# Two transformer blocks in one kernel: inputs loaded by features, the normalization applied after the first projections, another order of the in-projections

## The chip, the cores and the metric

The kernel runs on one core of a Trainium2 chip. A core has five engines that work side by side, each with its own in-order queue: TensorE (PE; the loading of its stationary operand is listed as PEld), VectorE (DVE), ScalarE (ACT), GpSimd (POOL) and SyncE (SP, which here only issues DMAs). The metric is the device time of one execution in microseconds. The same program before the change takes 843.48 us in the median of three runs (843.4 to 843.89).

## What is computed

Two transformer blocks on one sequence of 256 positions with 1024 features, all in float32. In the first block a Mamba-style branch (`ssd`) and a gated linear recurrence (`lru`) are fed from one in-projection, then follows a convolutional feed-forward stage. The second block has a delta-rule branch, a spatial gating branch, a sliding-window attention and an attention to a memory of 256 rows. Cut to what the change touches:

```python
def rmsnorm(x, w):
    y = x * rsqrt(mean(x * x, -1) + 1e-6)
    return y * w

def first_block(x, ...):
    h = rmsnorm(x, mix_pre_norm)
    u_z, u_xbc, u_dt, u_ly, u_lx, u_g = split(h @ w_in)
    y_a = ssd_mixer(u_z, u_xbc, u_dt, ...)     # conv, scan, times silu(u_z), grouped norm
    y_b = rglru_mixer(u_ly, u_lx, ...)         # recurrence over conv(u_lx), times gelu(u_ly)
    g = sigmoid(u_g + gate_b)
    x = x + rmsnorm((g0 * (y_a @ w_proj_ssm) + g1 * (y_b @ w_proj_lru)) @ w_out, ...)
    ...                                        # feed-forward
def second_block(x, mem, ...):
    cols = rmsnorm(x, norm_pre) @ w_in_2
    mem_kv = rmsnorm(mem, norm_mem) @ w_mem_kv
    # delta branch: q, k are divided by their norm over the 128 features of a head;
    # in chunks: solve (I + L) u = rhs with L strictly lower triangular
    ...
```

## The kernel before

**Precision.** Every big product is done in three passes on numbers split into a high and a low part (`mm3`: high by high, high by low, low by high). The weights come from memory as halves of 512 KB (`Weights`): `load` brings one into one of three raw buffers, `_split` lets ACT cast it to the high part (`whi`, L112) and DVE subtract that for the low part (`wlo`, L113), into one of five pairs of buffers. Activations are kept by features (features on the partitions, positions along the free dimension), as `HH` and `HL`.

**Projections.** `proj_fm` makes 256 output features for all 256 positions: 48 matmuls of 256 columns. `proj_tm` makes 512 output features by positions: 48 matmuls of 512 columns. A projection asks for its weights with `W.next`, which also splits the halves up to five ahead. The PSUM pool `pp` has four banks for them.

**The order of PE.** `block1` and `block2` are the main program. It yields after each 12 matmuls of 256 columns or 6 of 512 columns. `Weave` counts these yields as steps, and after each lets one side program (two in the second block) put its next piece of PE work in between. A side program yields either a number of steps to wait, or the name of an event and a number of steps behind it; `yield "name"` in the main program is a join, which forces whatever is left of a side program at once. So PE's order is written out by hand, step by step. ACT's and DVE's order is chosen by the framework's planner, except inside `manual_schedule` in `program()`, where it is as written. SP's order is the planner's too.

**Start.** `program()` normalizes X by positions into `h0` (`norm_tm`: squares on ACT, root, reciprocal, scaling on DVE), transposes it with 16 PE transposes (`to_fm`) and evicts each feature tile into `HH` (ACT, times the norm's weight) and `HL` (DVE). In the same stretch it splits the first five weight halves, and casts the small weights (`small_w`).

**Block 1.** The in-projections run in the order `xbc` (4, 5, 0 to 3), `z`, `lx`, `ly`, then the gates `g0` to `g3`. Beside them run the side programs: `side_dt`; `side_ssd`, which transposes x (`pxt`), waits for the event `z`, and then makes a decay matrix (`pe`, three Exp on ACT) and every second step two heads (`py`); `side_gn`, the grouped norm, after `ssd` and `z`; `side_lru`, from the event `ssd` on, with eight pairs of products `pg` that read the buffer `lw`. The bias `gb` of the gates is loaded into that same buffer once the last `pg` has read it, and DVE adds it to each gate tile as it evicts it (L905). `side_mem` normalizes, transposes and splits the memory input while `pb` runs.

**Block 2.** `side_delta` sums the squares of q and k with four groups of `pss` products (one column each), makes `L` (`pkk`), and calls `diagonal()`: POOL inverts the diagonal blocks of 32 by 62 small instructions, with DMAs to memory and back to re-lay them before and after. `yield 30` then leaves 30 steps to it before the products `pit`, `piy`, `pix` (the doubling of the blocks), `pvn`, `pS`, `pr`, `pq` and `po1`. The main program joins `delta` behind the gates `g230` and `g231`, ahead of the product `up3`.

The lines that matter most for what follows:

```python
            diagonal()
            yield 30
...
                if p == 3:
                    yield ("z", 1)
...
            if p == 3:
                gb = big.tile([P, 2 * D], F32, tag="lw", name="gb")
                with tc.issue_after(W.loaded.ins):
                    nc.sync.dma_start(gb, gbias)
```

Of the kernel before, what the change touches and what calls it, by code (L numbers as in the profile page):

```python
# [8 lines left out]
F32 = mybir.dt.float32  # L9
# [57 lines left out]
class Weights:  # L67
# [48 lines left out]

    def next(self, kt=8):
# [63 lines left out]
def two_blocks_kernel(  # L181
    ctx: ExitStack,
    tc: tile.TileContext,
    x: bass.AP,
    mem: bass.AP,
    pcol: bass.AP,
# [73 lines left out]
    nc.sync.dma_start(wsmall, wsm.rearrange("p (k c) -> p k c", k=8))  # L260
    W.load(3)
    pr = cp.tile([P, NROW], F32, name="pr")
    nc.sync.dma_start(pr, prow)
# [304 lines left out]

    lamc = COL["lru_lambda"]
# [14 lines left out]
    def side_dt():  # L584

        yield 7
# [33 lines left out]
    def side_ssd():  # L620
# [42 lines left out]
        for h in range(-4, 18):  # L663
            if h < 0:
                p = h + 4
                yield (f"xs{p}", 7)

                pt = bank(f"pxt{p}")
                for tt in range(2):
                    for i in range(2):  # L670
                        nc.tensor.transpose(
                            pt[:, tt * S + i * P : tt * S + (i + 1) * P],
                            XS[:, 2 * p + i, tt * P : (tt + 1) * P], ident)
                for tt in range(2):
# [12 lines left out]
            yield 1  # L687
# [64 lines left out]
    def side_gn():  # L752
# [3 lines left out]
        SZ = ya["sz"]  # L756
        sq = tmp("gnsq")
# [40 lines left out]
    def side_mem():  # L798
# [7 lines left out]
        EL = act8("b5", "EL", F32R)  # L806
        for tt in range(2):
# [53 lines left out]
    def block1(HH, HL):  # L861

        for p in (4, 5, 0, 1, 2, 3):
            ps, _ = yield from proj_fm(f"xbc{p}", HH, HL, p == 4)
# [30 lines left out]
        wv.event("ly")  # L895
# [99 lines left out]
    def block2(HH, HL, MK, MV):  # L995
# [127 lines left out]
        def side_delta():  # L1123

            for a in range(2):
                for p in range(2):
                    yield (f"dn{a}{p}", 10)
                    sq = sqs[a, p]
                    pss = bank(f"pss{a}{p}")
                    for j in range(2):  # L1130
                        for tt in range(2):
                            i = 2 * j + tt
                            nc.tensor.matmul(pss[:, i : i + 1], sq[:, j, tt * P : (tt + 1) * P],
                                             one[:, 0:1], start=True, stop=True)
                    nc.vector.tensor_copy(
                        rn[:, a, :, 2 * p : 2 * p + 2],
                        pss[:, 0:4].rearrange("p (j t) -> p t j", j=2))
# [48 lines left out]
            yield 30  # L1186
# [424 lines left out]
    def program():  # L1611
        h0 = big.tile([P, 2, D], F32, tag="b2", name="h0")
# [15 lines left out]
    with tc.manual_schedule(engines={nc.tensor.engine}):  # L1628
        wv.add("dt", side_dt())
# [9 lines left out]
    "x", "mem", "pcol", "prow", "wsm", "lruw", "wsT", "lvl", "post", "gbias", "w_in", "w_pa", "w_pb",  # L1639
# [4 lines left out]
def _layout(inp):  # L1644
# [15 lines left out]
    d = {"x": a("x")[0], "mem": a("mem_2")[0]}  # L1660
    d["post"] = np.stack([
# [20 lines left out]
    d["w_in"] = np.concatenate([xbc, tiles(wz), tiles(wlx), tiles(wy), tiles(wg, 512)])  # L1682
# [80 lines left out]
```

## Time and profile before

| | before |
|---|---|
| median of three runs | 843.48 us |
| profiled execution, its own time | 844.04 us |
| span of the profiled execution | 842.3 us |
| mean granted TensorE clock | 0.993 |
| PE busy | 819.2 us, 97% |
| PEld busy | 749.4 us, 89% |
| DVE busy | 593.8 us, 70% |
| ACT busy | 511.9 us, 61% |
| POOL busy | 53.4 us, 6% |
| read from memory | 142.84 MB, 171 GB/s over the span |

The span runs from the first to the last instruction of the core; an execution's own time is a little longer. A busy share is an average over the whole span: an engine with 70% can still be the one that is late in a stage. The granted clock is the share of the full TensorE clock of 2.4 GHz that the chip allowed; 0.50 of it is 1.2 GHz. Matmuls are pipelined: one takes 0.28 us from start to end while the next starts 0.12 us behind it, so what counts is the distance of the starts.

### The profile page before, as it was taken

What the parts mean: (1) busy time and instruction counts of PE and PEld (TensorE: products, weight loads), DVE (VectorE), ACT (ScalarE), POOL (GpSimd) and SP (SyncE); (2) the same over time, 40 slices, a digit from 0 to 9 for tenths busy, and PEclk for the clock granted to TensorE, in tenths of its full rate; (3) what the DMA queues carried; (4) which work ended last, traced back from release to release, by engine and by line L of the source; (5) the groups of instructions that cost most, each with busy time, mean ns of one, the idle gap of its engine ahead of it and who ended that gap; (6) DMA issues with size and microseconds to landing.
All of it is one profiled execution on the core that took longest, in us unless ns stands there. A gap on an engine that the chain in (4) does not pass through costs nothing.

```text
span 842.3 us, 14020 instructions
## 1 busy us (share of the span) xinstructions
PE 819.2 (97%) x5464; PEld 749.4 (89%) x5464; DVE 593.8 (70%) x973; ACT 511.9 (61%) x777; POOL 53.4 (6%) x97
## 2 busy tenths in 40 slices
PE   6999999999999999999999999999779999999997
PEld 5999899888889999999889899998779988888886
DVE  6896974996778788888743787766545666466673
ACT  7675768884556655655643478856736665544452
POOL 0000000000000000000000100048710000000000
PEclk9999999999999999999999999999979999999999
DMA  7755344656754665565665464454604346666551
GB/s 247 260 168 159 121 151 126 203 192 207 253 169 152 206 194 179 176 196 179 207 194 195 132 227 143 152 159 127 178 10 150 104 148 200 200 200 195 181 199 51
DMA packets 40387, 145.07 MB, mean 172 GB/s; under 512 B 4673, under 2 KB 4929, under 8 KB 40065
## 3 DMA queue, kind: packets, MB, share of 16 engines
q1 hardware_dynamic: 39600, 142.73, 53.2%
q0 software_dynamic: 576, 0.92, 0.6%
q8 instruction: 43, 0.70, 0.3%
q10 hardware_dynamic: 144, 0.52, 0.2%
q14 instruction: 24, 0.19, 0.1%
HBM read 142.84 MB, written 1.31 MB: 171 GB/s over the span
## 4 chain that ended last, share of the span: by engine, by line
PE 89%; POOL 5%; DMA 2%; DVE 2%; issue 1%; ACT 1%; DVEq 0%; POOLq 0%
PE fu L399 5%; PE fu L398 5%; PE fu L400 5%; PE g L398 5%; PE g L399 5%; PE g L400 5%; PE z L398 3%; PE fd L398 3%; PE fd L399 3%; PE fd L400 3%; PE z L399 2%; PE z L400 2%; POOL bM L1113 2%; POOL bM L1109 2%; PE up L399 2%; PE up L398 2%
## 5 line engine op out<-in xcount | busy, mean ns | idle before, releaser
L113 DVE TENSOR_TENSOR wlo<-wraw,whi 128x1024 fp32r<-128x1024 f32 x258 | 314.9, 1227 | 153.1 <-ACT whi L112 151.1
L112 ACT CAST whi<-wraw 128x1024 fp32r<-128x1024 f32 x258 | 268.7, 1050 | 218.1 <-PE fu L399 48.5
L398 PE MATMUL fu<-HH,whi 128*128 128x256 f32 x384 | 108.7, 283 | 0.0
L399 PE MATMUL fu<-HL,whi 128*128 128x256 f32 x384 | 108.7, 283 | 0.0
L400 PE MATMUL fu<-HH,wlo 128*128 128x256 f32 x384 | 108.7, 283 | 0.0
L398 PE MATMUL g<-whi,HH 128*128 128x512 f32 x192 | 75.9, 395 | 0.0
L400 PE MATMUL g<-whi,HL 128*128 128x512 f32 x192 | 74.8, 390 | 0.0
L399 PE MATMUL g<-wlo,HH 128*128 128x512 f32 x192 | 74.7, 389 | 0.0
L398 PEld LDWEIGHTS fu<-HH,whi 128*128 128x128 f32 x384 | 73.7, 192 | 0.0
L399 PEld LDWEIGHTS fu<-HL,whi 128*128 128x128 f32 x384 | 73.7, 192 | 0.0
L400 PEld LDWEIGHTS fu<-HH,wlo 128*128 128x128 f32 x384 | 73.7, 192 | 0.0
L398 PE MATMUL z<-HH,whi 128*128 128x256 f32 x192 | 57.2, 298 | 0.0
L399 PE MATMUL z<-HL,whi 128*128 128x256 f32 x192 | 54.7, 285 | 0.0
L400 PE MATMUL z<-HH,wlo 128*128 128x256 f32 x192 | 54.7, 285 | 0.0
L560 DVE SCALAR_TENSOR_TENSOR fc<-fu,pc,fc 128x255 f32<-128x255 f32 (+1 forms) x96 | 43.7, 478 | 1.6
L400 PEld LDWEIGHTS g<-whi,HL 128*128 128x128 f32 x192 | 36.0, 188 | 7.6
L398 PEld LDWEIGHTS g<-whi,HH 128*128 128x128 f32 x192 | 36.1, 188 | 7.3
L399 PEld LDWEIGHTS g<-wlo,HH 128*128 128x128 f32 x192 | 36.1, 188 | 7.3
L399 PE MATMUL fd<-wlo,FH 128*128 128x512 f32 (+1 forms) x120 | 41.7, 347 | 0.0
L398 PE MATMUL fd<-whi,FH 128*128 128x512 f32 (+1 forms) x120 | 41.6, 347 | 0.0
L400 PE MATMUL fd<-whi,FL 128*128 128x512 f32 (+1 forms) x120 | 41.6, 347 | 0.0
L398 PEld LDWEIGHTS z<-HH,whi 128*128 128x128 f32 x192 | 37.2, 194 | 0.8 <-issue 0.7
(522 smaller groups left out, 2026.2 us busy)
## 6 DMA issues: line engine op xcount, KB each, us to landing
wraw<-in_w_in_dram SPq DMA_DIRECT2D x130, 512.0 KB, 3.9
wraw<-in_w_fu_dram SPq DMA_DIRECT2D x48, 512.0 KB, 3.8
wraw<-in_w_fd_dram SPq DMA_DIRECT2D x24, 512.0 KB, 3.8
wraw<-in_w_o_dram SPq DMA_DIRECT2D x16, 512.0 KB, 3.9
wraw<-in_w_up_dram SPq DMA_DIRECT2D x16, 512.0 KB, 3.5
wraw<-in_w_pa_dram SPq DMA_DIRECT2D x8, 512.0 KB, 3.5
wraw<-in_w_pb_dram SPq DMA_DIRECT2D x8, 512.0 KB, 4.4
wraw<-in_w_mk_dram SPq DMA_DIRECT2D x4, 512.0 KB, 4.2
```

Of the source, the lines that this page charges most:

```text
L112: nc.scalar.copy(hi, raw)
L113: nc.vector.tensor_tensor(out=lo, in0=raw, in1=hi.bitcast(F32), op=ALU.subtract)
L398: nc.tensor.matmul(o, wh, xh, start=first, stop=False)
L399: nc.tensor.matmul(o, wh, xl, start=False, stop=False)
L400: nc.tensor.matmul(o, wl, xh, start=False, stop=last)
L560: nc.vector.scalar_tensor_tensor(o[:, d:S], in0=p[:, 0 : S - d], scalar=col(wname, (taps - 1 - d) * n + i), in1=o[:, d:S], op0=ALU.mult, o ...
L1109: eng.tensor_tensor(out=t, in0=xb[:, j : j + 1, :].to_broadcast([P, n, 8]), in1=lb[:, j, j + 1 : 32].unsqueeze(2).to_broadcast([P, n, 8]), ...
L1113: eng.tensor_tensor(out=xb[:, j + 1 : 32, :], in0=xb[:, j + 1 : 32, :], in1=t, op=ALU.subtract)
```

## The change

The layout on the host adds X and the memory input a second time, by features (`xT`, `memT`, two halves each).

- **Start.** X by features comes first, each half followed by a weight half; X by positions, most of the column constants, the small weights and the row constants come behind them (`more_loads`). The first two weight halves are split in four pieces each (`split_pieces`), and behind each piece one feature tile of X, not normalized, is multiplied with the norm's weight and split into `HU` and `LU` (`feature`). The squares of X by positions follow behind the fourth half, and give the factor of each position.
- **Order of block 1.** The four `ly` projections come first, made from `HU` and `LU`; the factor is applied to their result, when they are evicted (DVE, times `rbc`). The new side program `side_rms` spreads the factors over the partitions with two small matmuls into `rbc`, and DVE multiplies X by features with it in four steps, each followed by the split of two feature tiles into `HH` and `HL`. All later projections use those.
- **ssd, z.** The heads of `side_ssd` no longer wait for the event `z`; z is evicted with a plain copy and Silu is applied in `side_gn`.
- **Memory.** `side_mem` loads the memory by positions (for the squares) and by features; two small matmuls spread the factors, POOL multiplies (two feature tiles at a time), ACT and DVE split. The transposes go.
- **Norms on quarters.** The sums of squares of four heads are made by four matmuls on 32-column quarters of the array, copied and transposed.
- **Doubling later.** `yield 30` becomes `yield 44`.

```diff
+    def split_pieces(self, n):
...
+        for i in range(n):
+            q = slice(i * w, (i + 1) * w)
+            nc.scalar.copy(hi[:, q], raw[:, q])
+            nc.vector.tensor_tensor(out=lo[:, q], in0=raw[:, q], in1=hi[:, q].bitcast(F32),
+                                    op=ALU.subtract)
+            yield
+        self.load(j + 1 + self.raw_bufs)
...
-    nc.sync.dma_start(X[:, 0, :], x[0:P, :])
-    nc.scalar.dma_start(X[:, 1, :], x[P : 2 * P, :])
     pc = cp.tile([P, NCOL], F32, name="pc")
-    nc.sync.dma_start(pc, pcol)
-    W.load(2)
+    nc.scalar.dma_start(pc[:, 0:8], pcol[:, 0:8])
+    XT = act8("b2", "XT")
+    for g in range(2):
+        nc.sync.dma_start(XT[:, 4 * g : 4 * g + 4, :],
+                          xT[g].rearrange("p (k t) -> p k t", k=4))
+        W.load(g + 1)
+    W.load(3)
...
+    def more_loads(i):
+        if i == 0:
+            for tt in range(2):
+                nc.sync.dma_start(X[:, tt, :], x[tt * P : (tt + 1) * P, :])
+        else:
+            nc.sync.dma_start(pc[:, 8:NCOL], pcol[:, 8:NCOL])
+            nc.sync.dma_start(wsmall, wsm.rearrange("p (k c) -> p k c", k=8))
+            nc.sync.dma_start(pr, prow)
...
+    def feature(k, src, hi, lo):
+        w = col("mix_pre_norm", k)
+        nc.scalar.activation(hi[:, k, :], src[:, k, :], AF.Identity, scale=w)
+        nc.vector.scalar_tensor_tensor(
+            lo[:, k, :], in0=src[:, k, :], scalar=w, in1=hi[:, k, :].bitcast(F32),
+            op0=ALU.mult, op1=ALU.subtract)
...
+    def side_rms():
+        yield 6
+        ps = bank("prx")
+        for tt in range(2):
+            nc.tensor.matmul(ps[:, tt * P : (tt + 1) * P], rx[:, tt : tt + 1].to_broadcast([P, P]),
+                             ident, start=True, stop=True)
+        nc.scalar.copy(rbc, ps[:, 0:S])
+        wv.event("rms")
+        y = act8("b7", "xn")
+        for g in range(4):
+            yield 1
+            q = slice(2 * g, 2 * g + 2)
+            nc.vector.tensor_tensor(out=y[:, q, :], in0=XT[:, q, :],
+                                    in1=rbc.unsqueeze(1).to_broadcast([P, 2, S]), op=ALU.mult)
+            for k in (2 * g, 2 * g + 1):
+                feature(k, y, HH, HL)
+        wv.event("h")
...
     def side_dt():
-        yield 7
+        yield ("h", 5)
...
                 if p == 3:
-                    yield ("z", 1)
+                    yield 1
...
         SZ = ya["sz"]
+        for hf in range(2):
+            q = slice(4 * hf, 4 * hf + 4)
+            nc.scalar.activation(SZ[:, q, :], SZ[:, q, :], AF.Silu)
...
+        MT = act8("b0", "MT")
+        for g in range(2):
+            nc.sync.dma_start(MT[:, 4 * g : 4 * g + 4, :],
+                              memT[g].rearrange("p (k t) -> p k t", k=4))
...
-            norm_tm(MEM[:, tt, :], MEM[:, tt, :], f"mem{tt}")
-        yield 10
-        yield from to_fm(MEM, EH, EL, "norm_mem_2", "mem", 1)
+            nc.scalar.activation(MEM[:, tt, :], MEM[:, tt, :], AF.Square,
+                                 accum_out=rm[:, tt : tt + 1])
...
+                nc.gpsimd.tensor_tensor(out=MT[:, q, :], in0=MT[:, q, :],
+                                        in1=rmb.unsqueeze(1).to_broadcast([P, 2, S]), op=ALU.mult)
...
     def block1(HH, HL):
+        late = []
+        for p in range(4):
+            ps, b = yield from proj_fm(f"ly{p}", HU, LU, p == 0)
+            late.append((p, ps, b))
+            while late and "rms" in wv.events:
...
+            yield
+        wv.event("ly")
...
-            nc.scalar.activation(SZ[:, 2 * p : 2 * p + 2, :], b, AF.Silu)
+            nc.scalar.copy(SZ[:, 2 * p : 2 * p + 2, :], b)
...
             wv.event(f"lx{p}")
-            yield
-        for p in range(4):
-            _, b = yield from proj_fm(f"ly{p}", HH, HL)
-            nc.scalar.copy(GY[:, 2 * p : 2 * p + 2, :], b)
             if p == 3:
                 gb = big.tile([P, 2 * D], F32, tag="lw", name="gb")
...
         def side_delta():
-                for p in range(2):
-                    yield (f"dn{a}{p}", 10)
...
+                yield (f"dn{a}1", 10)
+                pss = bank(f"pss{a}")
+                for h in range(4):
+                    nc.tensor.matmul(pss[32 * h : 32 * h + 32, 0:S], one[:, 0:32],
+                                     sqs[a, h // 2][:, h % 2, :], start=True, stop=True,
+                                     tile_position=(0, 32 * h))
+                f = sm.tile([P, S], F32, tag="spf", name=f"ss{a}", bufs=1)
+                nc.vector.tensor_copy(f, pss[:, 0:S])
+                yield 3
...
             diagonal()
-            yield 30
+            yield 44
...
     def program():
...
-            for tt in range(2):
-                norm_tm(h0[:, tt, :], X[:, tt, :], f"n1{tt}", True)
-            W.split(1)
-            for _ in to_fm(h0, HH, HL, "mix_pre_norm", "n1", 0,
-                           lambda b: W.split((1, 2, 2, 4)[b])):
-                pass
+            for g in range(2):
+                for k, _ in enumerate(W.split_pieces(4)):
+                    feature(4 * g + k, XT, HU, LU)
+                more_loads(g)
+            W.split(4)
+            for tt in range(2):
+                nc.scalar.activation(NRM[:, 0:1024], X[:, tt, :], AF.Square,
+                                     accum_out=rx[:, tt : tt + 1])
+            nc.scalar.activation(rx, rx, AF.Sqrt, bias=eps1, scale=1.0 / D)
+            nc.vector.reciprocal(rx, rx)
```

## Rows read from the trace of the kernel before

**Rows 1.** The page, first part: busy us (share of the span) xinstructions

```profile
PE 819.2 (97%) x5464; PEld 749.4 (89%) x5464; DVE 593.8 (70%) x973; ACT 511.9 (61%) x777; POOL 53.4 (6%) x97
```

**Rows 2.** Timeline of PE: start us, us, engine, line, instruction, xcount [idle us before <-releaser]

```profile
7.97 3.39 PE L488 MATMUL n_t<-ident,h 128*128 128x128 f32 x16 [7.97 <-DVE h L478]
...
11.78 0.39 PE L399 MATMUL xbc<-HL,whi 128*128 128x256 f32 x1 [0.31 <-DVE HL L498]
...
615.09 1.94 PE L1200 MATMUL pit<-bXY,bLA 128*128 128x64 f32 x8 [8.67 <-DMA bXY<-dx]
```

**Rows 3.** Windows: us, busy us of PE, PEld, DVE, ACT, POOL, granted clock, DMA share, GB/s

```profile
610.00:612.00 2.00, 0.00 (x0) 0.00 (x0) 0.00 (x0) 0.00 (x0) 0.30 (x1) 0.93 0.35 143
620.00:622.00 2.00, 2.00 (x11) 1.56 (x11) 0.00 (x0) 0.00 (x0) 0.00 (x0) 0.52 0.00 0
```

**Rows 4.** Timeline of PE, 256-column matmuls early and behind the hole

```profile
12.47 0.28 PE L398 MATMUL xbc<-HH,whi 128*128 128x256 f32 x1
12.59 0.28 PE L399 MATMUL xbc<-HL,whi 128*128 128x256 f32 x1
...
619.17 0.41 PE L398 MATMUL z<-HH,whi 128*128 128x256 f32 x1
619.38 0.41 PE L399 MATMUL z<-HL,whi 128*128 128x256 f32 x1
```

**Rows 5.** Timeline of POOL, first and last DMA round of the solve

```profile
550.29 2.47 POOL L1097 DMA_DIRECT2D dl<-bLA  x4 [62.30 <-DVE XPB L1431]
...
611.70 2.33 POOL L1121 DMA_DIRECT2D bXY<-dx  x4 [4.47 <-DMA dx<-bM]
```

**Rows 6.** Chain that ended last: start us, us, what (one fp32 matmul may be two records)

```profile
82.16 0.80 PE py L655 x8
...
226.94 0.87 PE mem_t L488 x8
...
507.96 0.79 PE pss L1133 x8
...
540.61 0.92 PE pkk L1170 x4
```

**Rows 7.** Timeline of POOL, two instructions of the solve, 144 columns each

```profile
582.17 1.29 POOL L1109 TENSOR_TENSOR bM<-bM,bXY 128x144 f32<-128x144 f32 x1
583.54 0.50 POOL L1113 TENSOR_TENSOR bM<-bM 128x144 f32<-128x144 f32 x1
```

**Rows 8.** Timeline of DVE: a weight split, low parts of features, 512 columns

```profile
9.51 1.22 DVE L113 TENSOR_TENSOR wlo<-wraw,whi 128x1024 fp32r<-128x1024 f32 x1
...
11.25 1.66 DVE L498 SCALAR_TENSOR_TENSOR HL<-n_t,pc,HH 128x256 fp32r<-128x256 f32 x4 [0.52 <-ACT HH L496]
...
114.62 0.68 DVE L761 TENSOR_TENSOR XS<-XS,SZ 128x512 f32<-128x512 f32 x1
```

**Rows 9.** Timeline of ACT: the first square of X, high parts of features

```profile
5.63 1.06 ACT L465 ACTIVATE h<-X 128x1024 f32<-128x1024 f32 x1 [2.90 <-DMA X<-in_x_dram]
...
10.38 1.57 ACT L496 ACTIVATE HH<-n_t,pc 128x256 fp32r<-128x256 f32 x4 [0.96 <-PE n_t L488]
```

**Rows 10.** Windows, columns as in rows 3: the first loads

```profile
3.00:6.00 3.00, 0.00 (x0) 0.00 (x0) 0.20 (x2) 0.37 (x1) 0.00 (x0) 1.00 1.00 399
```

**Rows 11.** Windows, columns as in rows 3: the stage of the xbc projections

```profile
30.00:40.00 10.00, 10.00 (x83) 9.89 (x83) 9.75 (x20) 7.24 (x9) 0.00 (x0) 1.00 0.89 315
```

**Rows 12.** Timeline of PE: the first matmuls of gate projection g2

```profile
164.62 0.39 PE L398 MATMUL g<-whi,HH 128*128 128x512 f32 x1
164.85 0.39 PE L399 MATMUL g<-wlo,HH 128*128 128x512 f32 x1
```

**Rows 13.** Timelines of SP and DVE: the load of gb, its first use

```profile
152.52 0.33 SPq L893 DMA_DIRECT2D gb<-in_gbias_dram  x1
...
158.82 1.28 DVE L905 TENSOR_TENSOR G<-g,gb 128x512 f32<-128x512 f32 x2
```

**Rows 14.** DMA issues: tensors, queue, xcount, KB each, median us to landing

```profile
gb<-in_gbias_dram SPq DMA_DIRECT2D x1, 1024.0 KB, 4.9
```

More of the change, by code (lines that the diff above doesn't have):

```diff
@@ L115, in _split @@
             self.ns += 1
+    def split_pieces(self, n):
+        nc, j, w = self.nc, self.ns, HW // n
+        raw = self.raw.pop(j)
+        hi = self.pool.tile([P, HW], F32R, tag="whi", name=f"whi{j}", bufs=self.bufs)
+        lo = self.pool.tile([P, HW], F32R, tag="wlo", name=f"wlo{j}", bufs=self.bufs)
+        self.hl[j] = (hi, lo)
+        self.ns += 1
+        for i in range(n):
[5 more added lines that the diff above has]
+        self.load(j + 1 + self.raw_bufs)
     def next(self, kt=8):
@@ L184, in two_blocks_kernel @@
     x: bass.AP,
+    xT: bass.AP,
     mem: bass.AP,
+    memT: bass.AP,
     pcol: bass.AP,
@@ L567, in two_blocks_kernel @@
     wv = Weave(1)
+    HU = act8("b3", "HU", F32R)
+    LU = act8("b6", "LU", F32R)
+    NRM = big.tile([P, 2048], F32, tag="b5", name="NRM")
+    rbc = NRM[:, 1024 : 1024 + S]
+    rx = sm.tile([P, 2], F32, name="rx", bufs=1)
+    def feature(k, src, hi, lo):
[21 more added lines that the diff above has]
+        wv.event("h")
     lamc = COL["lru_lambda"]
@@ L806, in side_mem @@
         EL = act8("b5", "EL", F32R)
+        rm = sm.tile([P, 2], F32, name="rm", bufs=1)
         for tt in range(2):
-            norm_tm(MEM[:, tt, :], MEM[:, tt, :], f"mem{tt}")
-        yield 10
-        yield from to_fm(MEM, EH, EL, "norm_mem_2", "mem", 1)
+            nc.scalar.activation(MEM[:, tt, :], MEM[:, tt, :], AF.Square,
+                                 accum_out=rm[:, tt : tt + 1])
+        nc.scalar.activation(rm, rm, AF.Sqrt, bias=eps1, scale=1.0 / D)
+        nc.vector.reciprocal(rm, rm)
+        yield 8
+        ps = bank("prm")
+        for tt in range(2):
+            nc.tensor.matmul(ps[:, tt * P : (tt + 1) * P], rm[:, tt : tt + 1].to_broadcast([P, P]),
+                             ident, start=True, stop=True)
+        rmb = MEM[:, 0, 0:S]
+        nc.scalar.copy(rmb, ps[:, 0:S])
+        for k in range(8):
+            w = col("norm_mem_2", k)
+            if k % 2 == 0:
+                q = slice(k, k + 2)
+                nc.gpsimd.tensor_tensor(out=MT[:, q, :], in0=MT[:, q, :],
+                                        in1=rmb.unsqueeze(1).to_broadcast([P, 2, S]), op=ALU.mult)
+            nc.scalar.activation(EH[:, k, :], MT[:, k, :], AF.Identity, scale=w)
+            nc.vector.scalar_tensor_tensor(
+                EL[:, k, :], in0=MT[:, k, :], scalar=w, in1=EH[:, k, :].bitcast(F32),
+                op0=ALU.mult, op1=ALU.subtract)
         em["h"], em["l"] = EH, EL
@@ L861, in block1 @@
     def block1(HH, HL):
+        late = []
[3 more added lines that the diff above has]
+            while late and "rms" in wv.events:
+                i, ps, b = late.pop(0)
+                o = GY[:, 2 * i : 2 * i + 2, :]
+                if b is not None:
+                    nc.vector.tensor_tensor(
+                        out=o, in0=b, in1=rbc.unsqueeze(1).to_broadcast([P, 2, S]), op=ALU.mult)
+                    continue
+                for j in range(2):
+                    nc.vector.tensor_tensor(out=o[:, j, :], in0=ps[j], in1=rbc, op=ALU.mult)
+            yield
+        assert not late
+        wv.event("ly")
         for p in (4, 5, 0, 1, 2, 3):
-            ps, _ = yield from proj_fm(f"xbc{p}", HH, HL, p == 4)
+            ps, _ = yield from proj_fm(f"xbc{p}", HH, HL)
             two = (2 * p, 2 * p + 1)
@@ L1125, in side_delta @@
             for a in range(2):
-                for p in range(2):
-                    yield (f"dn{a}{p}", 10)
-                    sq = sqs[a, p]
-                    pss = bank(f"pss{a}{p}")
-                    for j in range(2):
-                        for tt in range(2):
[L1132 to L1137, printed above, removed]
+                yield (f"dn{a}1", 10)
[7 more added lines that the diff above has]
+                yield 3
+                pst = bank(f"psst{a}")
+                for tt in range(2):
+                    t = slice(tt * P, (tt + 1) * P)
+                    nc.tensor.transpose(pst[:, t], f[:, t], ident)
+                nc.vector.tensor_copy(
+                    rn[:, a], pst[:, 0:S].rearrange("p (t h c) -> p t h c", t=2, c=32)[:, :, :, 0])
             sk, rq = rn[:, 0], rn[:, 1]
@@ L1628, in two_blocks_kernel @@
     with tc.manual_schedule(engines={nc.tensor.engine}):
+        wv.add("rms", side_rms())
         wv.add("dt", side_dt())
@@ L1638 @@
 _ARGS = (
-    "x", "mem", "pcol", "prow", "wsm", "lruw", "wsT", "lvl", "post", "gbias", "w_in", "w_pa", "w_pb",
+    "x", "xT", "mem", "memT", "pcol", "prow", "wsm", "lruw", "wsT", "lvl", "post", "gbias", "w_in", "w_pa", "w_pb",
     "w_o", "w_mk", "w_mv", "w_fu", "w_fd", "w_in2", "w_up2", "w_o2",
@@ L1660, in _layout @@
     d = {"x": a("x")[0], "mem": a("mem_2")[0]}
+    d["xT"] = d["x"].T.reshape(2, 4, P, S).transpose(0, 2, 1, 3).reshape(2, P, 4 * S)
+    d["memT"] = d["mem"].T.reshape(2, 4, P, S).transpose(0, 2, 1, 3).reshape(2, P, 4 * S)
     d["post"] = np.stack([
@@ L1681, in _layout @@
     xbc = tiles(wx)[[4, 5, 0, 1, 2, 3]]
-    d["w_in"] = np.concatenate([xbc, tiles(wz), tiles(wlx), tiles(wy), tiles(wg, 512)])
+    d["w_in"] = np.concatenate([tiles(wy), xbc, tiles(wz), tiles(wlx), tiles(wg, 512)])
     d["w_pa"] = tiles(a("w_proj_ssm")[0], 512)
```

5 lines of the change are left out of this document (removed).

## The prediction

> **What bounds the kernel now.** I read the page's first part: TensorE (PE) is busy for 819.2 us of a span of 842.3 us [rows 1], so only what PE waits for or no longer has to do can move the end. Then PE's timeline, for its idle rows. There are only two of size: 7.97 us ahead of its first instruction, and 8.67 us ahead of the matmul `pit` of the second block's delta side [rows 2]. Elsewhere the matmuls follow each other without a hole, so ScalarE (ACT), VectorE (DVE) and the weight loads keep up everywhere else. The second hole costs more than its length. The granted clock is 0.93 in 610 to 612 us and 0.52 in 620 to 622 us [rows 3]: between the levels of 2.4 and 1.2 GHz those shares mean that it falls near 611.7 and is back near 621.9 us. At the low level a 256-column matmul starts every 0.21 us, at the high one every 0.12 us [rows 4]. That `pit` waits for the small triangular solve on GpSimd (POOL) and its four rounds of DMA, which start at 550.29 us and whose last loads are issued at 611.70 us [rows 5]. PE runs through the 30 program steps (one `yield` of the main program each) that the code leaves for it between 550 and 606 us, 1.9 us a step.
>
> **The change, part by part.**
>
> (a) "Doubling later", 30 to 44 steps. Every later piece of the delta side comes 14 steps later. At 1.4 us (twelve 256-column matmuls of 0.12) to 1.9 us a step that is 20 to 27 us of other PE work, and 8.7 are wanted. So the hole goes: 8.67 us. With it goes the slow stretch behind it, 615.1 to 621.9 us: 6.8 x (1 - 0.12/0.21) = 2.9 us. Sum **11.6 us gained**. The cover is the z and gate projections, which are there anyway. What comes late next is the delta side's own end: counted step by step, its last product `po1` was due 11 steps ahead of the forced join in front of `up3`, and 14 steps later it is forced at the join, one step (1.4 us) behind `pvn1`. Between them DVE has to evict `pvn1` (512 columns, as in the 0.68 us row) behind at most one weight split of 1.22 us [rows 8]: **0.5 us lost**, 0 to 1.5.
>
> (b) The memory input loaded by features. Sixteen PE transposes go, two groups of 0.87 us [rows 6]; two full float32 matmuls of 128 columns come. A float32 matmul of 256 columns takes 0.43 us (two in the 0.92 us row less its overlap) [rows 6], so these take 0.21 us each. **Gain 1.3 us.** DMAs: SP issues 1 MB more (`MT`) behind `MEM`; weights are five halves ahead there, so nothing waits for it. POOL gets four multiplications of 128x512. In the solve two of its instructions of the same 144 columns take 0.50 and 1.29 us, 0.8 apart [rows 7]. So the new ones take 1.8 us each by width, up to 2.6, about 10 us in all; the split features are wanted 25 us later. Cost 0; if DVE loses the 0.8 us four times in return, 3 us, the five halves in hand still cover most of it, so at most 1. The Trainium skill ("SBUF — State Buffer", Who interferes with whom) says that a DVE instruction with two SBUF inputs and a GpSimd one that reads SBUF exclude each other for a whole instruction; the long row agrees with it. By that rule DVE could be held for most of the 10 us, and the sum would be 1 us worse or more.
>
> (c) Norms on quarters. Four groups of `pss`, 0.8 us each [rows 6], 3.2 us, go. In come, twice, four float32 matmuls of 256 columns on 32-column quarters of the array and two transposes (0.22 us). One after another the four take 1.7 us, side by side 0.43. The nearest row is `py`, four matmuls on 64-column halves, 0.80 us [rows 6] where the widths add up to 1.28: part of the overlap. I take 0.7. **Gain 3.2 - 1.8 = 1.4 us**, between -0.7 and 1.9. The Trainium skill ("TensorEngine Tiling (Array Packing)", Theoretical Speedup) states up to 4x for 32-column tiles. The `py` row falls short of the 2x that it states for halves. By the page the gain would be 1.9 us.
>
> (d) The start. Before, X (1.05 MB) lands at 5.6 us [rows 9], and the queue moves 399 GB/s from 3 us on [rows 10], 1.04 MB by then; then squares, scaling, transposes and eviction follow, and the stream proper starts at 11.8 us. After, X by features and the first weight half are 1.05 MB at the head of the queue: again 5.7 us. ACT and DVE then split k-slices in turn. A 128x256 piece takes ACT 0.4 us [rows 9] and DVE 0.4 [rows 8] in a row of four, two on each engine per slice, 0.75 us a slice. The first slice is complete at 7.0 us, the eighth at 12.3 us; PE begins on the first at 6.6 us. It starts at the low clock level (as the second hole shows it takes it some 6 to 7 us of work behind an idle stretch to get back, while before the change it had done so by 12 us, 4 us after its first transpose; I take 3.9 us): three slices at 6 x 0.21 = 1.28 us, the rest at 0.72 us. The first 48 matmuls end at 14.1 us instead of 11.8 + 48 x 0.12 = 17.6 us: **3.5 us gained**, if nothing follows. Three things follow. Two small matmuls for the row factors: 0.4 us. X by positions comes only behind the fourth weight half, which waits for the first one's split (9.1 us): 2 us until data flow and 1.6 MB at 399 GB/s make 15.2 us. ACT's written order then puts the second square (1.3 us), the root, the small weights and the Exp table load (3 us together, an estimate) ahead of the fifth half's cast, which ends near 20.5 us (1.0), its DVE part near 21.7 us (1.2, [rows 8]); projection `ly2` wants it at 20.4 us: 1.3 us. Then, from 20.6 us, DVE owes five weight splits (5.7), eight slices scaled (2.4) and split (3.0) and the late evictions (1.9), 13.0 us, and PE wants most of it by 32 to 33 us; DVE has 0.25 us free in 10 us of the next stage [rows 11]: 1.0 us, 0 to 4. **Net 0.8 us gained**, between -3 and 3.1.
>
> (e) LRU gate first. The projections `ly` go from the end of the in-projections to the front. So xbc, its events and the ssd side come 16 steps later. The ssd side regains 10 by no longer waiting for z, and starts 6 steps later than before, measured from the gate projections `g0` to `g3`, which stay in place. Its successors move by 6 as well: the eight `pg` products, and the load of `gb` into the buffer they read. Before, `gb` is issued at 152.52 us, right behind the last `pg`, lands 4.9 us later [rows 14], and DVE adds it to the first two gate tiles from 158.82 us, 0.6 us each [rows 13], which frees the PSUM bank that `g2` needs. `g2` starts at 164.62 us [rows 12], 5.1 us behind the first of them. Six steps of 1.37 us (six 512-column matmuls of 0.23, [rows 12]) are 8.2 us, so PE **waits 2.6 us**: 3.1 if DVE is as late as before, 1.8 if at once, and from 0 to 6 in all, since SP holds the later weights behind that load. The rest of the LRU chain had more room. z evicted without Silu saves ACT table swaps; the two wide Silus come in the same 13 us ahead of `pgn` and cost nothing if ACT runs them early. SP's other moved loads are in (d).
>
> **Sum**: 11.6 - 0.5 + 1.3 + 1.4 + 0.8 - 2.6 = 12.0 us. The profiled execution took 844.04 us (span 842.3 and 1.7 around it), 0.56 above the median of the runs: 832.0 on its footing, **831.5 us** on the median's.
>
> **The rivals.** A: the start runs clean and `gb` is hidden. Then (d) is 3.1 and (e) 0: 826.6 us. For it: PE tolerates lateness, five halves are in hand. Against: DVE at 9.75 of 10 us [rows 11]. B: the start is lost to DVE (-3) and the `gb` wait takes 5: 837.7 us. C: the change doesn't do what it says at `pit`: the hole reappears, with its slow clock, because POOL's chain stretches by as much as the 14 steps. Then only the small parts stay: 843.1 us. Against it: nothing is added to that chain. D, slower: the feed of the first projections is so thin that PE stays at the low level through all four `ly`. The point is a slice taking ACT and DVE over 1.28 us instead of 0.75; then 4 x 48 matmuls cost 0.09 us more each, 17 us, and the end is 849 us. Against it: the row costs of (d) are well below.
>
> **How the numbers follow.** Forecast 0.62 (own range 828 to 835.5), A 0.14, B 0.16, C 0.04, D 0.04. The range 825.5 to 838 takes in A and most of B and leaves out C, D and tails. A measurement here tells about 0.2%, 1.7 us, from no change: faster 0.92, same 0.04, slower 0.04.
>
> **What would show it.** (a) no idle row ahead of `pit`, clock 1.00 around it; `po1` right behind `pvn1` at the join. (b), (c) `mem_t` gone, `pss` near 0.7 us a group. (d) first matmul of `ly` near 6.5 us, last of `ly0` near 14, idle rows at `ly2` and ahead of xbc4. (e) an idle row ahead of `g2` whose releaser is the DVE add of `gb`. Wrong if the hole at `pit` stays, or if the in-projections end over 4 us later than the sum has it.

## The result and the profile after

The changed kernel takes 833.67 us in the median of four runs (833.08 to 833.77), the kernel before 843.68 beside it: 0.9874 of the time, 95% interval 0.9856 to 0.9892. The prediction had said 831.5 us, range 825.5 to 838. The profiled execution took 833.6 us (span 831.9), 10.4 us less than that of before; between the medians it is 10.0.

The first part of the page, after (before: [rows 1]):

```profile
PE 813.5 (98%) x5428; PEld 741.5 (89%) x5428; DVE 599.3 (72%) x980; ACT 519.9 (62%) x791; POOL 61.1 (7%) x101
```

PE's timeline after, all idle rows above 0.25 us and the first products of the doubling (columns as in [rows 2]):

```profile
7.03 0.58 PE L425 MATMUL ly<-HU,whi 128*128 128x256 f32 x1 [7.03 <-ACT HU L605]
...
22.34 0.38 PE L427 MATMUL ly<-HU,wlo 128*128 128x256 f32 x1 [0.30 <-DVE wlo L113]
...
59.58 0.70 PE L687 MATMUL pcb<-bBC 128*128 128x256 f32 x2 [0.58 <-ACT bBC L972]
...
167.38 0.50 PE L425 MATMUL g<-whi,HH 128*128 128x512 f32 x1 [3.03 <-DVE G L1003]
...
522.18 0.44 PE L1236 MATMUL psst<-ident,ss 128*128 128x128 f32 x2 [0.93 <-DVE ss L1231]
...
635.17 1.00 PE L1301 MATMUL pit<-bXY,bLA 128*128 128x64 f32 x8
```

The 8.67 us ahead of `pit` [rows 2] are gone. Four waits have come: 0.30, 0.58, 3.03 and 0.93 us. Windows of the stretch where the clock had fallen [rows 3], after; PE is busy throughout and the granted clock is 1.00:

```profile
610.00:612.00 2.00, 2.00 (x18) 1.48 (x17) 0.86 (x4) 0.00 (x0) 0.00 (x0) 1.00 0.92 306
620.00:622.00 2.00, 2.00 (x19) 2.00 (x19) 1.46 (x3) 1.77 (x2) 0.00 (x0) 1.00 0.89 268
```

POOL's last loads of the solve are issued 1.7 us later than before [rows 5], as all of PE's work there is (`gv` in the table below), and now 22 us ahead of `pit`:

```profile
613.38 2.32 POOL L1219 DMA_DIRECT2D bXY<-dx  x4 [4.66 <-DMA dx<-bM]
```

Most of PE's products are in both kernels, and ahead of each point below the same of them are done. So the start of a product that both have tells how far one kernel is ahead there. The table has this, in us against the kernel before (minus is earlier), for the profiled executions of the changed kernel and of three of the experiments:

| first product of | before, at | changed | only_later | no_start | four |
|---|---|---|---|---|---|
| `pa` (behind the gates) | 186.38 | +2.93 | +0.07 | +0.05 | -2.79 |
| `o` | 232.66 | +1.61 | +0.07 | -1.28 | -3.79 |
| `mk` | 255.69 | +2.03 | +0.07 | -0.88 | -3.40 |
| `gv` (behind the norms) | 569.09 | +1.61 | +0.09 | -1.27 | -4.98 |
| `up3` (behind the join) | 702.61 | -10.81 | -12.34 | -13.69 | -17.27 |
| end of the span | 842.3 | -10.4 | -12.2 | -13.7 | -17.1 |

### The profile page after: what moved, and what is told of

It reads as the page before. It is cut to its first block, busy times and chain, and to the rows that moved or that the text cites. A ratio compares the mean times of both kernels' runs of the same rounds, so it can differ in the third digit from the quotient of the medians.

```text
span 831.9 us, 13970 instructions
## 1 busy us (share of the span) xinstructions
PE 813.5 (98%) x5428; PEld 741.5 (89%) x5428; DVE 599.3 (72%) x980; ACT 519.9 (62%) x791; POOL 61.1 (7%) x101
## 4 chain that ended last, share of the span: by engine, by line
PE 92%; DVE 4%; DMA 2%; ACT 1%; issue 0%; DVEq 0%; SPq 0%; ACTq 0%
PE fu L427 6%; PE fu L426 6%; PE fu L425 6%; PE g L425 5%; PE g L427 5%; PE g L426 5%; PE z L425 3%; PE z L426 3%; PE z L427 3%; PE fd L426 3%; PE fd L425 3%; PE fd L427 3%; PE up L427 2%; PE up L425 2%; PE up L426 2%; PE o L427 2%
## 5 line engine op out<-in xcount | busy, mean ns | idle before, releaser
L425 PEld LDWEIGHTS g<-whi,HH 128*128 128x128 f32 x192 | 36.1, 188 | 10.6 <-DVE G L1003 3.5
```

The lines of the kernel that those rows point to most:

```text
L425: nc.tensor.matmul(o, wh, xh, start=first, stop=False)
```

## The experiments

The theory after the comparison: the doubling alone brings 12.4 us, memory and norms 1.3 together, and the new start with the new order costs 2.9, because what it gains is 0.1 us up to `g2` and `gb` then costs 3.0. The rivals are that the new start is what helps, or that the doubling needs the other parts.

**only_later**: the kernel before with one line changed.

```diff
-            yield 30
+            yield 44
```

> The kernel before with one edit: 44 steps instead of 30 behind the small triangular solve. Theory 1 (read from the trace after the whole change: from the first gv product to the first up3 product it takes 12.4 us less): the same 12.4 us come from this edit alone, 831.3 us. Theory 2 (the prediction's sum): 8.67 us of hole and 2.9 us of slow stretch, less 0.5 us at the forced join, 832.6 us. Rival: the solve begins earlier in the changed kernel because the norms take less time, and without that a part of the hole of 1 to 2 us is left ahead of pit: 833 us or more, with an idle row there.

Measured 831.8 us (831.62 to 832.0), ratio 0.9857 (0.9844 to 0.9871). From `gv` to `up3` it takes 12.43 us less, as the changed kernel does (12.42), and nothing is idle at `pit`. The median lies between the two theories; the trace decides for the first, and the rival is out. This one line brings 1.9 us more than the whole change, and the runs of the two don't overlap.

**no_start**: the kernel before with three hunks of the change.

```diff
-        yield from to_fm(MEM, EH, EL, "norm_mem_2", "mem", 1)
...
+        ps = bank("prm")
...
-                    pss = bank(f"pss{a}{p}")
...
+                pss = bank(f"pss{a}")
...
-            yield 30
+            yield 44
```

> The kernel before with three of the parts: 44 steps, the memory input by features, the norms on quarters; start and order of the in-projections as before. Theory 1: the new start and order cost 2.9 us net in the changed kernel (0.1 us gained up to g2, 3.0 us waited there for gb), so this kernel is faster than the fully changed one by about 3: 830.3 us. Theory 2 (the prediction's sum): start and order cost 1.8 us net, 829.7 us on its terms. Rival: the new start gains 3 us as a whole and something else made the sum short: 836 us or more. In the trace: no idle row at g2, about 0.9 us idle ahead of psst as in the changed kernel.

Measured 830.6 us (830.33 to 830.91), ratio 0.9843 (0.983 to 0.9856): 3.1 us less than the changed kernel. The new start and order cost that much net. At `psst` PE waits 0.93 us here too, so that wait belongs to the norms.

**gb_apart**: the changed kernel, `gb` in two halves.

```diff
+            if p == 2:
+                ga = big.tile([P, D], F32, tag="wrow", name="ga")
...
+                    nc.sync.dma_start(ga, gbias[:, 0:D])
...
-                nc.vector.tensor_tensor(out=g, in0=ps, in1=gb[:, 512 * i : 512 * i + 512],
+                nc.vector.tensor_tensor(out=g, in0=ps, in1=(ga, gb)[n][:, 512 * c : 512 * c + 512],
```

> The changed kernel, with the first half of gb (all that the tiles of g0 and g1 need) in a buffer of its own that is free then, loaded two projections earlier; the second half stays where gb was. Theory 1: the 3.03 us that PE waits ahead of g2 go and nothing takes their place, 830.6 us. Rival 1: DVE or ACT, which carry the recurrence of the lru branch in the same stretch, are late next and take 2 us of it back: 832.6 us, with an idle row ahead of g2 or pa whose releaser is not the DMA chain. Rival 2: the earlier load delays weights: an idle row ahead of lx3 or g0.

Measured 830.33 us (829.54 to 831.0), ratio 0.9837 (0.9824 to 0.9851): 3.3 us less than the changed kernel. No idle row at `g2`; `pa` starts 1.42 us ahead of before instead of 2.93 behind. That is 4.35 us, and 1.0 of it isn't the edit's: `g0` starts at 134.07 us instead of 135.07, ahead of anything that the edit touches on PE (the last section shows how the start differs between executions). A part came back later: 0.64 us at `m1b`, where it had been 0.10, and 1.22 at `psst` instead of 0.93.

**warm**: the changed kernel with 21 matmuls on constants ahead of the first projection.

```diff
+            pw = bank("pwarm")
+            for _ in range(21):
+                nc.tensor.matmul(pw[:, 0:P], ident, ident, start=True, stop=True)
```

> The changed kernel, with 21 matmuls of 128 columns on constants ahead of the first projection, in the time in which PE has nothing to do. Theory 1: the first 25 matmuls of ly0 start 0.21 us apart because PE was idle before; with work ahead they start 0.12 us apart or wait for their slice (0.72 us each), the 49th matmul comes at 13.7 us instead of 15.45; then ly2 waits 2.0 us instead of 0.3 for its weights, whose cast stands behind the squares and the table load in ACT's order, and the time is 833.4 us, almost the same. Rival 1: the spacing changes at 12.5 us whatever PE did before: 49th matmul at 15.4 us. Rival 2: ly2 doesn't wait longer: 832.0 us.

Measured 839.72 us (838.62 to 841.44), ratio 0.9953 (0.9937 to 0.9969), 6 us more than the changed kernel. The 21 took 7.83 us, longer than I had thought, so `ly0` began at 9.12 us instead of 7.03. But its matmuls then start 0.12 us apart from the second one on, where the changed kernel's stay 0.21 us apart until 12.5 us: with work ahead the low level doesn't reach into `ly0` (first rival out), and `ly2` didn't wait (second rival right there). The 49th comes at 14.95 us. That is no clear gain: the changed kernel has it at 15.45, but five other runs with its start, without matmuls ahead, have it at 14.42 to 15.39. The loss stands elsewhere. PE's idle rows and the windows behind the first:

```profile
61.42 0.70 PE L687 MATMUL pcb<-bBC 128*128 128x256 f32 x2 [3.36 <-ACT bBC L972]
...
171.62 0.80 PE L425 MATMUL g<-whi,HH 128*128 128x512 f32 x1 [3.88 <-DVE G L1003]
```

```profile
61.00:64.00 3.00, 2.58 (x13) 2.53 (x14) 3.00 (x7) 2.74 (x5) 0.00 (x0) 0.70 0.99 399
64.00:67.00 3.00, 3.00 (x19) 2.82 (x18) 3.00 (x7) 0.10 (x1) 0.00 (x0) 0.73 0.44 158
67.00:70.00 3.00, 3.00 (x28) 3.00 (x27) 0.75 (x3) 1.24 (x2) 0.00 (x0) 1.00 0.62 175
```

ACT's timeline shows most of why `pcb` waits 3.36 us instead of 0.58: the planner, which chose ACT's order anew, put a weight cast ahead of the table load and of the Silu that `pcb` needs.

```profile
58.38 1.04 ACT L112 CAST whi<-wraw 128x1024 fp32r<-128x1024 f32 x1
59.45 1.28 ACT L972 ACT_TABLE_LOAD   x1
60.74 0.63 ACT L972 ACTIVATE bBC<-bBC 128x512 f32<-128x512 f32 x1
```

In the changed kernel the table load stands there too, but no cast right ahead of it:

```profile
57.60 1.28 ACT L972 ACT_TABLE_LOAD   x1 [0.23 <-DVE bBC L587]
58.89 0.63 ACT L972 ACTIVATE bBC<-bBC 128x512 f32<-128x512 f32 x1
```

So the Silu is 1.85 us later; the other 0.9 us of the longer wait is PE being at `pcb` that much earlier.

**short_warm**: 14 of these matmuls, and `pcb` later.

```diff
-        yield ("bc", 9)
+        yield ("bc", 13)
...
+            for _ in range(14):
```

> The changed kernel, with 14 instead of 21 matmuls of 128 columns ahead of the first projection (in the run with 21 each took 0.37 us at the low level, so 14 end near 6.8 us, where the first slice is ready), and with 13 instead of 9 steps between the event bc and the products pcb, so that these don't wait. Theory 1: all of ly0 runs at the high level or at the pace of its slices (0.72 us each), 49th matmul at 13.7 us instead of 15.45; ly2 waits about 1 us for its weights instead of 0.3; pcb waits no more (0.58): 832.1 us. Theory 2: what held the run with 21 back (3.4 us idle ahead of pcb and a fall of the clock behind it) was only the length of the extra work: 831.4 us. Rival: work ahead of the first projection makes the planner order ACT and DVE in another way, and a wait of over 2 us turns up at pcb, pxt or g2 beside the known 3.0: 834 us or more.

Measured 835.23 us (834.53 to 835.79), ratio 0.9893 (0.9872 to 0.9914), against 832.1 expected. Up to the end of xbc it went as theory 1 says: 49th matmul at 13.33 us, `pcb` without a wait, xbc done 1.7 us earlier than in the profiled execution of the changed kernel (`z` starts 0.4 us earlier than in later_37, whose low level ended sooner). Then PE waits 3.67 us for `gb` instead of 3.03, and the granted clock is low behind it, which the 3.03 us hadn't brought:

```profile
166.00:168.00 2.00, 1.69 (x4) 1.40 (x5) 2.00 (x5) 1.98 (x3) 0.00 (x0) 0.50 0.93 354
168.00:170.00 2.00, 2.00 (x6) 1.52 (x6) 2.00 (x3) 1.99 (x2) 0.00 (x0) 0.50 0.66 270
```

Twelve matmuls of 512 columns start 0.43 us apart instead of 0.23: 2.4 us. The rival's time came, though not by its mechanism: no new wait, but the known one with the clock behind it. That the 14 matmuls bring this isn't shown: mem_early, mem_dve and later_37 below have none of them and wait as long at `g2`, with a fall of the clock too.

**mem_early**: in `side_mem`, the changed kernel with

```diff
         nc.vector.reciprocal(rm, rm)
-        yield 8
+        yield 5
```

> The changed kernel, with the products prm and with them the four POOL multiplications of the memory input 3 steps (4.1 us) earlier. Theory 1: in the changed kernel the addition into MG takes 1.77 us instead of 0.68 because a POOL multiplication runs beside it, which makes m1b late and costs PE 0.1 us idle and some 0.3 beside it between o and mk; 3 steps earlier the POOL multiplications end ahead of that addition, it takes 0.68 us, and o to mk takes 23.0 us instead of 23.45: 0.4 us less in all, below what the time can show. Rival: the addition is long for another reason (the same length without POOL beside it), and o to mk stays at 23.45 us.

A single execution took 837.85 us; PE also waited 4.10 us at `g2` in it, so it is read by its stage. From `o` to `mk` it takes 25.03 us instead of 23.45. Theory 1 falls. `prm` now waits 0.57 us: the second square waits 0.87 us for the load of MEM (0.25 in the changed kernel), and a table load stands behind it. DVE's order has all eight low parts in a row, at first at POOL's pace, and two weight splits behind them, ahead of the addition that `m1b` needs (1.26 us idle). Timelines of ACT and DVE:

```profile
221.41 1.06 ACT L876 ACTIVATE MEM<-MEM 128x1024 f32<-128x1024 f32 x1 [0.87 <-DMA MEM<-in_mem_dram]
```

```profile
229.77 5.71 DVE L894 SCALAR_TENSOR_TENSOR EL<-MT,pc,EH 128x256 fp32r<-128x256 f32 x8
```

**mem_dve**: the changed kernel with the multiplications on DVE.

```diff
-                nc.gpsimd.tensor_tensor(out=MT[:, q, :], in0=MT[:, q, :],
+                nc.vector.tensor_tensor(out=MT[:, q, :], in0=MT[:, q, :],
```

> The changed kernel, with the four multiplications of the memory input on DVE instead of POOL. Theory 1: DVE instructions with two SBUF inputs are held up while POOL multiplies (in the changed kernel a weight split takes 1.62 us there instead of 1.22, the addition into MG 1.77 instead of 0.68); without POOL they take 1.22 and 0.68 us again, the four take 0.7 us each on DVE, and o to mk takes 23.05 us instead of 23.45. Rival: the long DVE instructions have another cause and stay long. Second rival: DVE's own 2.8 us more delay the addition into MG just as much, and o to mk takes 23.4 us or more.

A single execution took 836.27 us, with 3.54 us at `g2`. `o` to `mk` takes 23.04 us, as theory 1 says; the second rival falls. DVE's timeline of the changed kernel beside POOL's multiplications (228.13 to 235.29 us):

```profile
229.65 1.62 DVE L113 TENSOR_TENSOR wlo<-wraw,whi 128x1024 fp32r<-128x1024 f32 x1 [0.62 <-ACT whi L112]
...
231.79 0.91 DVE L894 SCALAR_TENSOR_TENSOR EL<-MT,pc,EH 128x256 fp32r<-128x256 f32 x1
232.63 0.68 DVE L1030 TENSOR_TENSOR G<-pb,G 128x512 f32<-128x512 f32 x1
...
234.06 1.77 DVE L1031 TENSOR_TENSOR MG<-MG,G 128x512 f32<-128x512 f32 x1
```

and of mem_dve:

```profile
230.27 1.23 DVE L113 TENSOR_TENSOR wlo<-wraw,whi 128x1024 fp32r<-128x1024 f32 x1 [1.49 <-ACT whi L112]
...
235.40 0.69 DVE L1031 TENSOR_TENSOR MG<-MG,G 128x512 f32<-128x512 f32 x1
```

The instructions with two inputs in SBUF are the long ones; the one that reads PSUM (`pb`) takes 0.68 us in the middle of it. POOL is held up as well: of its multiplications the two beside a weight split take 2.06 and 2.28 us, the other two 1.47 and 1.48, and in the trace of before the ten instructions of the solve that take over 1 us all have a weight split beside them. The Trainium skill ("SBUF — State Buffer", Who interferes with whom) says that a DVE instruction with two SBUF inputs contends with a GpSimd one that reads SBUF, and calls what they share an exclusive lock. `MG` ends half a microsecond behind the last multiplication, which agrees.

**later_37**: the changed kernel with

```diff
-            yield 44
+            yield 37
```

> The changed kernel with 37 steps instead of 44 behind the solve. In the changed kernel the solve's last loads are issued at 613.38 us and pit starts at 635.17; by the trace of before 8.67 us of hole are 4.6 steps of 1.9 us, so 35 steps should do. Theory 1: no idle row ahead of pit, the time within 1 us of the changed kernel's 833.7. Theory 2: the solve itself is later when the pieces around it move, and part of the hole (2 us or more) comes back: 836 us or more. What po1 cost at the forced join would come off too, 0.5 us by the prediction's sum.

A single execution took 835.08 us, with 3.82 us at `g2` and 1.53 at `psst`. From `gv` to `up3` it takes 12.52 us less than before, against 12.42 with 44 steps, and `pit` (623.69 us) doesn't wait. Seven steps more than before would have done, and what `po1` costs at the forced join is 0.1 us at most. Its time is 1.4 us above the changed kernel's median, outside what theory 1 said, and the stages put that at `g2` and `psst`, ahead of the edit.

**joined** and **joined_warm**: the edits of gb_apart and mem_early, `pcb` 13 steps behind `bc`, and the first two hunks below; joined_warm has also the 14 matmuls and the third hunk.

```diff
-                yield 3
+                yield 5
                 pst = bank(f"psst{a}")
...
-            yield 44
+            yield 42
...
             nc.vector.reciprocal(rx, rx)
+            W.split(5)
```

> The changed kernel, with the first half of gb in a buffer of its own, 5 instead of 3 steps ahead of the transposes psst (and 42 instead of 44 behind the solve, so that po1 comes where it did), 13 instead of 9 steps ahead of pcb, and prm 3 steps earlier. Theory 1: each idle row that the changed kernel has beside its first goes: 3.03 us at g2, 0.93 to 1.2 at psst, 0.58 at pcb, 0.4 around m1b: 4.9 us less than the changed kernel, 828.7 us, and 1.6 us less than with gb apart alone. Rival: DVE is what is late, and a wait that is taken away comes back as long at the next place that needs DVE: 830.3 us, as with gb apart alone.

> The kernel with the four waits taken away, and beside that 14 matmuls ahead of the first projection and the fifth weight half cast ahead of the small weights and the table load. Theory 1: 1.7 us less than without these two, since ly0 loses nothing to the low level and ly2 doesn't wait: 827.0 us. Rival: what ly0 gains, DVE can't follow (it owes 13 us of work from 20 us on): waits of the same length at xbc, and 828.7 us.

Measured 831.66 us (830.84 to 832.12), ratio 0.9852 (0.9834 to 0.9869), and 830.5 us (829.65 to 832.45), ratio 0.9841 (0.982 to 0.9861); 828.7 and 827.0 were expected. The waits at `g2`, `psst` and `pcb` went, as theory 1 says. `prm` now waits 1.92 and 1.05 us, and `m1b` 1.56 and 1.72: the earlier `prm` again. The start brought 1.2 us between the two medians, whose runs overlap, and 0.7 us by the start of `pa`; 1.7 was expected.

**four** and **four_dve**: joined_warm with the step of mem_early taken back; four_dve has also the edit of mem_dve.

```diff
-        yield 5
+        yield 8
         ps = bank("prm")
```

> The kernel joined_warm, but with prm 8 steps behind the squares as in the changed kernel: gb apart, psst 5 steps, pcb 13 steps, 42 steps behind the solve, 14 matmuls ahead of the first projection and the fifth weight half cast early. Theory 1: what joined_warm lost between pb and mk (1.04 us idle at prm, 1.71 at m1b, 2.1 us in all against the kernel before, where the changed kernel gains 0.9) comes from the earlier prm alone, whose squares and POOL multiplications were not ready: 3.0 us less than joined_warm, 827.5 us. Rival: it comes from PE being earlier altogether, and stays: 830.5 us.

> The kernel four, with the four multiplications of the memory input on DVE instead of POOL. Theory 1: m1b doesn't wait (0.1 to 0.6 us with POOL): 0.4 us less than four, 827.1 us. Rival: DVE has no room for 2.8 us more there; 1 us or more above four.

Measured 827.35 us (826.96 to 827.85), ratio 0.9805 (0.9791 to 0.9819), and 827.78 us (826.64 to 828.63), ratio 0.9808 (0.9792 to 0.9824). Theory 1 of four holds: 6.3 us less than the changed kernel, about what the four waits (4.8 us) and the low clock of the start had taken. Between the two no difference can be told: on DVE `m1b` doesn't wait, but `n_t` and an `o` product do (0.63 and 0.27 us). PE's rows in four, first ones and the largest idle row behind them:

```profile
1.53 5.60 PE L1722 MATMUL pwarm<-ident 128*128 128x128 f32 x28 [1.53 <-POOL ident masks.py:199]
...
13.93 0.39 PE L427 MATMUL ly<-HU,wlo 128*128 128x256 f32 x1 [0.41 <-DVE wlo L113]
```

## Why the prediction came out right, and where its steps were off

It said 12.0 us of gain, 10.4 came between the profiled executions, and (a) carries it. The likeliest case came true, none of the rivals. That the sum is only 1.6 us off is partly luck: (a) was 1.3 us too low, the other terms together 2.9 too high. The terms, predicted and measured by the table above:

| step | predicted | measured |
|---|---|---|
| (a) doubling later, join | +11.1 | +12.4 |
| (b) memory by features | +1.3 | +0.9 |
| (c) norms on quarters | +1.4 | +0.4 |
| (d) start | +0.8 | +0.1 |
| (e) `gb` at `g2` | -2.6 | -3.0 |
| behind `up3` | 0 | -0.4 |

**(a)** The hole and the slow stretch were as worked out (8.67 and 2.9). The 0.5 us for `po1` at the join didn't come: `pvn1` starts at 688.72 us, one step of six products follows, then `po1` at 690.99, nothing idle. The other 0.8 us was not in the sum: `piy` and `pgs` together take 3.2 us instead of 4.5, of which the clock explains 0.4. In the new places two groups of `piy` no longer stand right ahead of `pgs`; that this is the reason is argued, not shown.

**(b)** The transposes brought 1.32 us by `o`, as predicted. The contention of POOL and DVE, bounded by 1 us there, took 0.4, and its place is the addition into `MG`, on which `m1b` waits; in mem_dve, without POOL, both are gone.

**(c)** The count of operations was right. PE's row of the first group, after:

```profile
515.68 0.64 PE L1227 MATMUL pss<-dsq,one 128*32 128x256 f32 x8
516.25 0.38 PE L425 MATMUL dn<-HH,whi 128*128 128x256 f32 x1
```

It takes 0.57 us of PE's time; 0.7 was taken, 1.7 would be four one after another, and the 4x that the Trainium skill names ("TensorEngine Tiling (Array Packing)", Theoretical Speedup) would be 0.43 by estimate, so most of the overlap is there. What the step left out is the wait: it costed two more operations for PE and forgot the copy between them on DVE. DVE's timeline:

```profile
518.67 1.21 DVE L113 TENSOR_TENSOR wlo<-wraw,whi 128x1024 fp32r<-128x1024 f32 x1
519.80 0.47 DVE L587 SCALAR_TENSOR_TENSOR KQ<-dn,pc,KQ 128x254 f32<-128x254 f32 x1
520.19 1.21 DVE L113 TENSOR_TENSOR wlo<-wraw,whi 128x1024 fp32r<-128x1024 f32 x1
521.33 0.47 DVE L587 SCALAR_TENSOR_TENSOR KQ<-dn,pc,KQ 128x253 f32<-128x253 f32 x1
521.72 0.41 DVE L1231 COPY ss<-pss 128x256 f32<-128x256 f32 x1
```

`pss` ends at 516.3 us, and the copy runs 5.4 us later behind DVE's queue of splits and convolutions; three steps reach to 521.25. So PE waits 0.93 us, the size of the miss; the second group doesn't wait. With five steps it is gone (joined, four).

**(d)** The first 48 matmuls gained 2.1 us (the 49th at 15.45 us against 17.51), not 3.5. Two sizes were off: the first starts at 7.03 us instead of 6.6, and the low level lasts until 12.5 us, 5.4 us of work, where I had taken 3.9 from a stretch of transposes. The second is this execution's: five other runs with the same start leave the low level after 3.2 to 5.5 us of work (last section), so no single figure was right. `prx` costs 0.36 (0.4 predicted), `ly2` waits 0.30 (1.3), and the late DVE and ACT show at `pcb` with 0.58 (1.0 at xbc4). That leaves 0.8; the other 0.7 is spread over the stages: `g0` to `g3` take 1.0 us more without the wait, `lx` 0.4 more, `py` 0.4 less. In the gates the second product behind a side piece can start 0.42 us behind the first instead of 0.23; before, that happens four times, after, six times, which is 0.4 of the 1.0 us. The 0.1 that is left of (d) hangs on the execution too: in gb_apart, with the same start and no wait at `g2`, `pa` is 1.4 us ahead of before. The lower end of the range, -3, isn't what its terms add up to: 3.5 - 0.4 - 1.3 - 4 is -2.2.

**(e)** The mechanism was right: `g2`, the DVE add and the six steps. The size was 0.4 off, since `gb` takes longer to land than before [rows 14]. DVE adds it as soon as it lands, which by the prediction's sum is 1.8 us; a landing 1.4 us later brings it to 3.0. DVE's row, SP's queue, after, and the DMA row:

```profile
166.63 2.49 DVE L1003 TENSOR_TENSOR G<-g,gb 128x512 f32<-128x512 f32 x4 [0.90 <-DMA gb<-in_gbias_dram]
```

```profile
160.25 0.33 SPq L992 DMA_DIRECT2D gb<-in_gbias_dram  x1
161.22 0.33 SPq L87 DMA_DIRECT2D wraw<-in_w_in_dram  x1
161.83 0.33 SPq L869 DMA_DIRECT2D MT<-in_memT_dram  x1
```

```profile
gb<-in_gbias_dram SPq DMA_DIRECT2D x1, 1024.0 KB, 6.4
```

A weight half and the first half of `MT`, a load that part (b) added, come 1 and 1.6 us behind it. I had put SP's new loads behind MEM, where "nothing waits for it"; the planner put `MT` ahead, beside `gb`. That these loads are what makes `gb` slow is argued, not shown: the half ahead of it is closer as well (1.2 us instead of 2.2), and no run changes one of these alone. In only_later, which has the block as before, `gb` takes 5.75 us.

Open: 0.3 us between the last product and the end of the span, and the 0.7 us of (d) one by one. No run has the new start without the new order of the projections, or one of the memory and the norms without the other; those are told apart by stages alone.

## What to carry to other kernels

A step that comes too early for its partner on another engine is worth looking for first: moving one number gave more than a rebuilt start. When an operation is cut into two on PE with a copy between, cost the queue of the engine that copies, not the copy. A load that reuses a buffer inherits the last reader's lateness; half of it in a free buffer gave back 3.3 us.

## What the runs showed of the hardware that was not expected

- Waits of nearly one length cost quite different times: behind 3.03 us at `g2` the granted clock stayed 1.00, behind 3.36 us at `pcb` (warm) it was 0.70 and 0.73, behind 3.67 us at `g2` (short_warm) 0.50, which cost 2.4 us on top.
- later_37 has the same order of instructions as the changed kernel up to the second block. Yet its `gb` took 7.1 us to land instead of 6.4, PE waited 3.82 us instead of 3.03, and the granted clock was 0.50 from 168 to 170 us. mem_early and mem_dve have that order up to 220 us as well: 7.4 and 6.9 us to land, 4.10 and 3.54 us of wait, and the clock falls in both. So the time of such a wait isn't fixed by the program, and of these four executions the one that stands for the changed kernel is the mildest. What short_warm and later_37 take above its 833.67 us can't be put down to their edits.
- At the start the column of the granted clock shows 1.00 while the products of 256 columns start 0.21 us apart, the distance of the low level [rows 4]; there the spacing tells the level, not the column. How long the low level lasts isn't fixed by the program either. With the same start it ends near 10.2 us in joined, 10.6 in later_37, 11.2 in mem_early, 11.9 in gb_apart and 12.5 in mem_dve and the changed kernel, while the first product starts between 6.88 and 7.03 us in all six. A window and PE's rows of the changed kernel, then those of later_37:

```profile
10.00:12.00 2.00, 2.00 (x12) 2.00 (x11) 2.00 (x6) 2.00 (x7) 0.00 (x0) 1.00 1.01 414
```

```profile
12.20 0.41 PE L426 MATMUL ly<-LU,whi 128*128 128x256 f32 x1
12.41 0.33 PE L427 MATMUL ly<-HU,wlo 128*128 128x256 f32 x1
12.58 0.28 PE L425 MATMUL ly<-HU,whi 128*128 128x256 f32 x1
12.70 0.28 PE L426 MATMUL ly<-LU,whi 128*128 128x256 f32 x1
```

```profile
10.34 0.40 PE L427 MATMUL ly<-HU,wlo 128*128 128x256 f32 x1
10.56 0.31 PE L425 MATMUL ly<-HU,whi 128*128 128x256 f32 x1
10.71 0.28 PE L426 MATMUL ly<-LU,whi 128*128 128x256 f32 x1
```
